# Four small changes of order in a two-layer trunk: x ahead of the first weights, a halving on ScalarE, copies ahead of low parts, mixing four places sooner

## The chip, the cores and the metric

The kernel runs on one core of one Trainium2 chip. The metric is the device time of one execution in microseconds (us), as the median of several runs. The profile is of one execution; its span is the time from the first to the last instruction that it shows. TensorE is PE (PEld its weight loads), VectorE DVE, ScalarE ACT, GpSimd POOL; SP issues nearly all DMAs.

## The reference

One sequence of 1024 tokens, width 1024, goes through two layers, all in fp32. Layer 0 mixes tokens with a gated MLP on one half of the width and a gated delta rule on the other; layer 1 with a differential attention. Both layers end with an MLP (width 4096, squared relu) and a gated embedding. What matters here is the start of layer 0 and the attention:

```python
hn = rms_norm(h, ln_mix_e[i])              # h = x
proj = hn @ w_in_e[i]                      # the first matmul
...
q = rms_norm(q.reshape(bsz, seq, C_HEADS, 2, C_HEAD_DIM), q_gain) * (C_HEAD_DIM ** -0.5)
k = rms_norm(k.reshape(bsz, seq, C_HEADS, 2, C_HEAD_DIM), k_gain)
slopes = alibi_slopes(C_HEADS)             # 2 ** -(1 .. 8) for the 8 heads
logits = jnp.einsum('bqhrd,bkhrd->bhrqk', q_blk, k) - slopes * dist
probs = softmax(where(dist >= 0, logits, -inf))
attn = probs[:, :, 0] - lam * probs[:, :, 1]
o = jnp.einsum('bhqk,bkhe->bqhe', attn, v)
h = h + rms_norm(o, sub_gain) * (1 - lam_init) @ w_out_o[i]
```

## The kernel before

Every fp32 operand of a large product is split into a rounded high part and the low rest, and a product is three matmuls (`mm3`: high by high, high by low, low by high). For a weight this is a DMA of a piece of 128 x 512 to `raw` (`Weight.load`, L103), a cast on ACT (L224) and a subtraction on DVE or POOL (L225). All instructions pass through a scheduler at build time, which orders each engine's instructions by the place at which the program emits them, by a model of when their operands are ready, and by what is marked as urgent; the order on each engine is then fixed. PE's matmuls all have line 78, its transposes line 81.

**Start.** `trunk` loads the first half of x (512 tokens) as two tiles of 128 x 2 x 1024, in four column pieces each (L2047, 256 KB a piece), and after each pair of pieces one of the four pieces of the first projection's weights (L2049, by L103). Below, these weight pieces are W0 to W3. `load_x` turns x by PE transposes into PSUM, eight times four of 128 x 128; ACT takes the scaled high part out of PSUM (L232), DVE the low part (L233), ACT also squares x for the norm (L849), and the turned x goes to memory by way of `xt` (L844, L845). Then come the second four weight pieces and all else that SP issues.

**Attention.** It works on 64 blocks, 8 heads by 8 blocks of 128 queries (block g is head g // 8, block b = g % 8 of it, with (b + 1) x 128 keys). One turn of the loop from L1212 on emits for block g the two logits (r = 0 and 1), the combination and the turning of block g - 1, the fetching of g - 2 and the values of g - 3.

- `logits`: two products into a PSUM bank (`qk`), one DVE instruction (L1065) that adds the table of distances `al` and keeps the row minimum `nm`, and an exponential on ACT (L1068). `al` is one SBUF tile of 128 x 1024; at the first block of each head it is multiplied by 0.5 in place (L1054), which gives the next head's slope.
- `begin` and `put_k`, `put_q`: a head's keys (queries) are turned by PE into one bank with the tag `tr`. ACT copies 64 partitions scaled (L1017; L1028 and L1029), then DVE writes the low part (L1018; L1030) from the same bank, for r = 0, and then the same for r = 1. ACT and DVE accesses of one PSUM bank are kept in the order in which the program emits them.
- Between these parts stand four calls of `pump` a turn. These are the numbered places: place i lies in block (i - 1) // 4. `pump` puts in a share of the projections for later heads as filler, by a table `MARKS` of (place, units done by then): 168 units are left when the loop starts, the last 16 are head 7's queries and keys. A unit is 12 matmuls of 256 columns; four units fill a bank with the tag `mm` (there are two), which is then evaluated by a square on ACT (L954), a sum and a root (L956 to L959) and two scalings on DVE (L963).
- From place 206 on (`TAIL`), `pump` also takes one step of `tails`: from 160 units on it turns the finished heads' outputs back (`put_halves`), and from 168 on it begins the output projection over heads 0 to 5 (`mix_part`, "mixing"): steps of six matmuls of 512 columns into an `mm` bank, whose weights are split by ACT and POOL and whose results are added to the residual on DVE (L1282). There are some 48 steps. What is left of them is emitted behind the loop, ahead of the rest of the output projection.

Of the kernel before, what the change touches and what calls it, by code (L numbers as in the profile page):

```python
# [13 lines left out]
AF = mybir.ActivationFunctionType  # L14
ALU = mybir.AluOpType
# [8 lines left out]
HT = 512  # L24
# [5 lines left out]
EARLY = 3000  # L30
LAG = 3
KA = (6, 5)
MARKS = ((64, 50), (192, 144), (212, 160), (227, 168))
TAIL = 205
LATE = {64: 5, 65: 2}
DIRECT = 61
# [5 lines left out]
def f32(ap):  # L42
    return ap.bitcast(F32)
# [73 lines left out]
class Trunk:  # L117
# [793 lines left out]
    def attention(self, w_qkv, w_out, gain_next, h_dram):  # L911

        nc = self.nc
        NB = NT
        hs, r = list(self.hs), list(self.r)
# [3 lines left out]
        al = self.slot("B", [P, S], F32, "al")  # L919
# [70 lines left out]
        half = (slice(0, 64), slice(64, P))  # L990
# [13 lines left out]
        def begin(hd):  # L1004

            qk = qks[hd]

            ks = self.slot(f"A{2 + hd % 2}", [P, 2, S], F32R, "ks")

            def put_k(hf):  # L1010
                pt = self.aux([P, HT], "tr", "tr")
                for t in range(4):
                    self.pe.transpose(pt[:, t * P : (t + 1) * P], qk[1][hf][:, t, :], self.ident)
                for r in range(2):
                    own, other = half[r], half[1 - r]
                    dst = ks[:, r, hf * HT : (hf + 1) * HT]
                    nc.scalar.activation(dst[own], pt[own], AF.Copy, scale=self.kg[own])  # L1017
                    nc.vector.scalar_tensor_tensor(dst[other], pt[own], self.kg[own], f32(dst[own]), ALU.mult, ALU.subtract)  # L1018

            def put_q(b2):  # L1020
                pt = self.aux([P, HT], "tr", "tr")
                for i in range(2):
                    self.pe.transpose(pt[:, i * P : (i + 1) * P], qk[0][b2 // 2][:, 2 * (b2 % 2) + i, :], self.ident)
                qh = self.slot(f"c{11 + b2 % 2}", [P, 2, 2 * P], F32R, "qh")
                ql = qlow[b2 % 2]
                for r in range(2):
                    own, other = half[r], half[1 - r]
                    nc.scalar.activation(qh[own, r], pt[own, 0 : 2 * P], AF.Copy, scale=self.qg[own])  # L1028
                    nc.scalar.activation(qh[other, r], pt[own, 0 : 2 * P], AF.Copy, scale=self.qg[own])  # L1029
                    nc.vector.scalar_tensor_tensor(ql[own, r], pt[own, 0 : 2 * P], self.qg[own], f32(qh[own, r]), ALU.mult, ALU.subtract)  # L1030
                return qh, ql

            put_k(0)
            heads[hd] = [ks, put_k, put_q, put_q(0)]

        class Block:
# [14 lines left out]
            def logits(me, r):  # L1051
                hd, b, n, nm, lg = me.hd, me.b, me.n, me.nm, me.lg[r]
                if b == 0 and r == 0:
                    nc.vector.tensor_scalar(al, al, 0.5, None, ALU.mult)  # L1054
                ks, _, _, (qh, ql) = heads[hd][:4]
                qs = slice((b % 2) * P, (b % 2 + 1) * P)
                nch = (n + HT - 1) // HT
                u0 = (NB - 1 - b) * P
                for c in range(nch):
                    k0, k1 = c * HT, min(n, (c + 1) * HT)  # L1060
                    ps = self.aux([P, HT], next(qk_tag), "qk")
                    self.pe.matmul(ps[:, : k1 - k0], lhsT=qh[:, r, qs], rhs=ks[:, r, k0:k1], start=True, stop=False)
                    self.pe.matmul(ps[:, : k1 - k0], lhsT=ql[:, r, qs], rhs=ks[:, r, k0:k1], start=False, stop=True)

                    nc.vector.tensor_tensor_reduce(  # L1065
                        out=lg[:, k0:k1], in0=ps[:, : k1 - k0], in1=al[:, u0 + k0 : u0 + k1], scale=-1.0,
                        scalar=3.0e38 if c == 0 else nm[:, r, 0:1], op0=ALU.add, op1=ALU.min, accum_out=nm[:, r, c : c + 1])
                nc.scalar.activation(lg[:, :n], lg[:, :n], AF.Exp, bias=nm[:, r, nch - 1 : nch], scale=-1.0, accum_out=me.sums[:, b, r : r + 1])  # L1068
# [107 lines left out]

        marks = [(0, 0), *MARKS]
        state = [0, 0]
# [852 lines left out]
def trunk(tc, x, p, ln_mix_e, w_in_e, gmlp_v_gain, gmlp_ws, gmlp_bs, gdn_conv, gdn_a_log, gdn_dt_bias, gdn_out_gain,  # L2031
          w_out_e, ln_mix_o, w_qkv_o, attn_q_gain, attn_k_gain, diff_lambda, attn_sub_gain, w_out_o, ln_mlp, w_mlp1,
          w_mlp2, ln_ple, w_ple_gate, w_ple_proj, masks, out):
    with ExitStack() as ctx:
        T = Trunk(tc, ctx)
        nc = tc.nc
# [4 lines left out]
        def rows(half):  # L2041
            tiles = [T.slot(("A1", "A2", "A4", "A5")[2 * half + u], [P, 2, D], F32, "x") for u in range(2)]
            n = 2 * D // HT if half == 0 else 2
            for c in range(n):
                cols = slice(c * D // n, (c + 1) * D // n)
                for u in range(2):
                    nc.sync.dma_start(tiles[u][:, :, cols], xs[half, u, :, :, cols])  # L2047
                if half == 0:
                    first.load()  # L2049
            return [tiles[t // 2][:, t % 2] for t in range(4)]  # L2050

# [7 lines left out]
        first = Weight(T, [(w_in_e[0][:, 1536:1792], 0)], KT, 256)  # L2059
        nc.scalar.dma_start(vr[0:8, 0:P], ln_mix_e[0].rearrange("(k p) -> k p", p=P))  # L2060
        x0 = rows(0)
        pt = T.aux_ps()
        T.pe.transpose(pt[:, 0:8], vr[0:8, 0:P], T.ident[0:8, 0:8])
# [9 lines left out]
        def rows_of_rest():  # L2073
            x1.extend(rows(1))
            vr = T.tmp()
            nc.vector.memset(vr[:, 0:P], 0.0)
            nc.sync.dma_start(vr[8:24, 0:P], ln_mlp.rearrange("l (k p) -> (l k) p", p=P))
            nc.sync.dma_start(vr[24:40, 0:P], ln_ple.rearrange("l (k p) -> (l k) p", p=P))
            nc.sync.dma_start(vr[40:48, 0:P], ln_mix_o[0].rearrange("(k p) -> k p", p=P))
            nc.sync.dma_start(vr[48:96, 0:P], gdn_conv[0].rearrange("t (m p) -> (t m) p", p=P))  # L2080
            nc.sync.dma_start(vr[96:100, 0:P], gmlp_bs[0])
            pt = T.aux_ps()
            T.pe.transpose(pt[:, 0:P], vr[:, 0:P], T.ident)
            nc.vector.tensor_copy(cols[:, 8:], pt[:, 8:P])
# [73 lines left out]
```

## Time and profile before

| | |
|---|---|
| timed runs, median (lowest to highest) | 2484.7 us (2482.77 to 2484.95) |
| the profiled execution | 2487.14 us |
| its span | 2485.4 us |
| DMA in it | 459.73 MB, mean 185 GB/s |
| the switch from head 6 to head 7 (`al` halved) | at 1627.9 us |
| mean granted clock of PE | 0.998 |

A row of a group gives line, engine, operation, output and input tiles, shapes and count, then busy time, mean ns of one, and idle time of the engine before them with what ended it. A row of the timeline gives start and length in us. In the chain each piece is what the next one waited for.

### The profile page before, as it was taken

What the parts mean: (1) busy time and instruction counts of PE and PEld (TensorE: products, weight loads), DVE (VectorE), ACT (ScalarE), POOL (GpSimd) and SP (SyncE); (2) the same over time, 40 slices, a digit from 0 to 9 for tenths busy, and PEclk for the clock granted to TensorE, in tenths of its full rate; (3) what the DMA queues carried; (4) which work ended last, traced back from release to release, by engine and by line L of the source; (5) the groups of instructions that cost most, each with busy time, mean ns of one, the idle gap of its engine ahead of it and who ended that gap; (6) DMA issues with size and microseconds to landing.
All of it is one profiled execution on the core that took longest, in us unless ns stands there. A gap on an engine that the chain in (4) does not pass through costs nothing.

```text
span 2485.4 us, 39881 instructions
## 1 busy us (share of the span) xinstructions
PE 2467.7 (99%) x13588; PEld 2106.4 (85%) x13588; DVE 1864.7 (75%) x3639; ACT 1291.2 (52%) x2591; POOL 324.0 (13%) x304
## 2 busy tenths in 40 slices
PE   9999999999999999999999999999999999999999
PEld 7998898888888887888899999988878888888887
DVE  7787877697667879566568888876886677787687
ACT  6553444464455435454366766664654555445553
POOL 0221331000000000000244443342000000000010
PEclk9999999999999999999999999999999999999999
DMA  8385645457556755553347776787465558657772
GB/s 246 114 255 118 172 150 178 140 175 245 161 178 238 256 184 191 187 173 115 119 97 171 163 173 153 192 215 245 155 218 192 180 185 288 215 182 218 231 245 86
DMA packets 539620, 459.73 MB, mean 185 GB/s; under 512 B 229524, under 2 KB 400920, under 8 KB 539416
## 3 DMA queue, kind: packets, MB, share of 16 engines
q1 hardware_dynamic: 513032, 451.93, 60.0%
q10 hardware_dynamic: 25360, 3.15, 0.8%
q0 software_dynamic: 1024, 2.10, 0.3%
q8 instruction: 107, 1.75, 0.3%
q14 instruction: 97, 0.79, 0.1%
HBM read 322.10 MB, written 134.96 MB: 184 GB/s over the span
## 4 chain that ended last, share of the span: by engine, by line
PE 93%; DVE 3%; DMA 2%; issue 1%; ACT 1%; SPq 0%; POOL 0%; DVEq 0%; ACTq 0%; POOLq 0%
PE mm L78 82%; PE po L78 3%; PE qk L78 3%; PE aux L78 2%; PE tr L81 1%; DMA raw<-in_w_mlp_dram 0%; DMA spill<-early 0%; PE pkq L78 0%; DVE raw L283 0%; PE pz L78 0%; PE py L78 0%; PE pks L78 0%; PE pgm L78 0%; PE pvn L78 0%; PE pab L81 0%
## 5 line engine op out<-in xcount | busy, mean ns | idle before, releaser
L224 ACT CAST w<-raw 128x512 fp32r<-128x512 f32 x598 | 365.0, 617 | 460.9 <-PE mm L78 387.0
L78 PE MATMUL mm<-g,w 128*128 128x512 f32 x2592 | 603.1, 394 | 1.0 <-DVE g L225 0.8
L78 PEld LDWEIGHTS mm<-g,w 128*128 128x128 f32 x2592 | 486.5, 188 | 115.2 <-DVE g L225 1.7
L78 PE MATMUL mm<-hi,w 128*128 128x512 f32 x1728 | 552.8, 397 | 0.0
L78 PE MATMUL mm<-w,hi 128*128 128x256 f32 (+2 forms) x2528 | 503.1, 294 | 1.4 <-ACT t L1585 1.0
L225 DVE TENSOR_TENSOR w<-raw,w 128x512 fp32r<-128x512 f32 (+1 forms) x510 | 346.6, 687 | 166.7 <-ACT w L224 156.4
L78 PEld LDWEIGHTS mm<-w,hi 128*128 128x128 f32 x2528 | 401.4, 188 | 16.5 <-ACT t L1585 1.2
L78 PEld LDWEIGHTS mm<-hi,w 128*128 128x128 f32 x1728 | 324.4, 188 | 73.6
L78 PE MATMUL mm<-w,lo 128*128 128x256 f32 (+2 forms) x1264 | 368.0, 292 | 0.0
L78 PE MATMUL mm<-lo,w 128*128 128x512 f32 x864 | 340.1, 394 | 0.0
L78 PE MATMUL mm<-t,w 128*128 128x512 f32 x1152 | 271.0, 394 | 0.4 <-ACT w L224 0.2
L78 PEld LDWEIGHTS mm<-t,w 128*128 128x128 f32 x1152 | 216.2, 188 | 51.9 <-DVE t L225 1.0
L78 PEld LDWEIGHTS mm<-w,lo 128*128 128x128 f32 x1264 | 237.8, 188 | 5.7
L78 PEld LDWEIGHTS mm<-lo,w 128*128 128x128 f32 x864 | 162.8, 188 | 36.6
L224 ACT CAST g<-graw 128x512 fp32r<-128x512 f32 x216 | 132.7, 617 | 43.2 <-DMA graw<-gd 16.4
L225 DVE TENSOR_TENSOR g<-graw,g 128x512 fp32r<-128x512 f32 x216 | 146.9, 684 | 9.9 <-DMA gd<-g 7.9
L1068 ACT ACTIVATE lg<-lg,nm 128x128 f32<-128x128 f32 (+7 forms) x128 | 99.2, 775 | 74.5 <-DVE nm L1065 73.5
L265 POOL TENSOR_TENSOR r<-ms,mhalf 128x4 f32<-128x4 f32 x12 | 12.5, 1043 | 943.1 <-DVE ms L263 916.5
L225 POOL TENSOR_TENSOR w<-raw,w 128x512 fp32r<-128x512 f32 (+1 forms) x88 | 116.0, 1336 | 138.2 <-ACT w L224 93.2
L349 ACT ACTIVATE g<-g 128x512 f32<-128x512 f32 x96 | 60.4, 632 | 110.8 <-DVE g L283 107.2
L1065 DVE CUSTOM_DVE_ANT_0 lg<-qk,al 128x512 f32<-128x512 f32 (+3 forms) x128 | 74.8, 587 | 27.6 <-PE qk L78 23.7
L78 PE MATMUL mm<-ohi,w 128*128 128x512 f32 x256 | 86.6, 401 | 0.0
(340 smaller groups left out, 3534.4 us busy)
## 6 DMA issues: line engine op xcount, KB each, us to landing
raw<-in_w_mlp_dram SPq DMA_DIRECT2D x352, 256.0 KB, 3.3
graw<-gd SPq DMA_DIRECT2D x224, 256.0 KB, 2.9
gd<-g SPq DMA_DIRECT2D x192, 256.0 KB, 3.2
raw<-in_w_ple_gate_dram SPq DMA_DIRECT2D x76, 256.0 KB, 3.5
acc<-h_dram SPq DMA_DIRECT2D x64, 256.0 KB, 4.3
keep<-in_w_mlp_dram SPq DMA_DIRECT2D x64, 256.0 KB, 4.3
raw<-in_w_in_e_dram SPq DMA_DIRECT2D x60, 256.0 KB, 3.7
h_dram<-acc SPq DMA_DIRECT2D x48, 256.0 KB, 2.8
```

What stands on the lines that cost most here:

```text
L78: self._next(self.engine.matmul(*a, **k))
L81: self._next(self.engine.transpose(*a, **k))
L224: self.nc.scalar.copy(hi, src)
L225: (lo_engine or self.nc.vector).tensor_tensor(lo, src, f32(hi), ALU.subtract)
L265: nc.gpsimd.tensor_tensor(r, ms, self.mhalf[:, 0:4], ALU.pow)
L349: nc.scalar.activation(g, src, AF.Relu)
L1065: nc.vector.tensor_tensor_reduce(out=lg[:, k0:k1], in0=ps[:, : k1 - k0], in1=al[:, u0 + k0 : u0 + k1], scale=-1.0, scalar=3.0e38 if c == 0 ...
L1068: nc.scalar.activation(lg[:, :n], lg[:, :n], AF.Exp, bias=nm[:, r, nch - 1 : nch], scale=-1.0, accum_out=me.sums[:, b, r : r + 1])
```

## The change

The first half of x is issued whole, and the four first weight pieces after it. The table of distances is halved by an ACT copy with scale 0.5 instead of a DVE multiplication. In `put_k` and `put_q` the copies of both r are emitted ahead of the low parts of both. The last entry of `MARKS` is (223, 168) instead of (227, 168), so the last eight units are done, and mixing begins, four places sooner.

```diff
-MARKS = ((64, 50), (192, 144), (212, 160), (227, 168))
+MARKS = ((64, 50), (192, 144), (212, 160), (223, 168))
...
                 for t in range(4):
                     self.pe.transpose(pt[:, t * P : (t + 1) * P], qk[1][hf][:, t, :], self.ident)
-                for r in range(2):
+                dsts = [ks[:, r, hf * HT : (hf + 1) * HT] for r in range(2)]
+                for own, dst in zip(half, dsts):
+                    nc.scalar.activation(dst[own], pt[own], AF.Copy, scale=self.kg[own])
+                for r, dst in enumerate(dsts):
                     own, other = half[r], half[1 - r]
-                    dst = ks[:, r, hf * HT : (hf + 1) * HT]
-                    nc.scalar.activation(dst[own], pt[own], AF.Copy, scale=self.kg[own])
                     nc.vector.scalar_tensor_tensor(dst[other], pt[own], self.kg[own], f32(dst[own]), ALU.mult, ALU.subtract)
...
                     nc.scalar.activation(qh[own, r], pt[own, 0 : 2 * P], AF.Copy, scale=self.qg[own])
                     nc.scalar.activation(qh[other, r], pt[own, 0 : 2 * P], AF.Copy, scale=self.qg[own])
+                for r, own in enumerate(half):
                     nc.vector.scalar_tensor_tensor(ql[own, r], pt[own, 0 : 2 * P], self.qg[own], f32(qh[own, r]), ALU.mult, ALU.subtract)
...
                 if b == 0 and r == 0:
-                    nc.vector.tensor_scalar(al, al, 0.5, None, ALU.mult)
+                    nc.scalar.activation(al, al, AF.Copy, scale=0.5)
...
                     nc.sync.dma_start(tiles[u][:, :, cols], xs[half, u, :, :, cols])
-                if half == 0:
+            if half == 0:
+                for _ in range(first.pieces):
                     first.load()
```

## The prediction, made before the result was known

> **What bounds the kernel now.** First the page's busy times, then the view of waits: what TensorE (PE) waited for, with us in total, times, longest.
>
> ```profile
> PE 2467.7 (99%) x13588; PEld 2106.4 (85%) x13588; DVE 1864.7 (75%) x3639; ACT 1291.2 (52%) x2591; POOL 324.0 (13%) x304
> ...
> PE aux L81 <- DMA x<-in_x_dram: 2.1, 1, 2.1
> PE tr L81 <- DVE ks L1018: 1.0, 1, 1.0
> PE qk L78 <- ACT qh L1029: 0.9, 1, 0.9
> PE po L78 <- DMA aT<-a_dram: 0.4, 1, 0.4
> PE tr L81 <- DMA ol<-o_dram: 0.3, 1, 0.3
> ```
>
> PE is busy in 2467.7 of 2485.4 us. No edit takes a matmul away, so an edit pays only where PE stands still or its clock is low. Of the 17.7 us of standing still, the places the diff can reach are these waits: the one for x at the start, and two in attention (1.0 and 0.9) that belong together. The table by stretches shows where:
>
> ```profile
> 1500.00:1600.00 100.00, 99.56 (x803) 97.28 (x802) 80.97 (x220) 67.02 (x173) 42.80 (x36) 1.00 0.72 169
> ...
> 1625.00:1630.00 5.00, 3.70 (x20) 2.56 (x18) 4.79 (x11) 3.22 (x9) 1.50 (x3) 1.00 0.83 252
> 1630.00:1635.00 5.00, 4.15 (x21) 4.05 (x22) 4.87 (x14) 3.46 (x12) 1.64 (x1) 0.66 0.89 140
> ```
>
> The columns are length, then busy time of PE, PEld, DVE, ACT and POOL, granted clock, DMA share, GB/s. PE loses 1.30 + 0.85 = 2.15 us in ten, while DVE is nearly full (4.79 and 4.87 of 5), and just behind it the clock is 0.66. This is the switch from head 6 to head 7, where the projections run out. The chain of waits there, and from the timeline the instructions that hold it (start, us, engine, line; in brackets the engine's idle time before it and what ended that):
>
> ```profile
> 1626.06 0.76 DVE ks L1018
> ...
> 1631.32 2.67 PE po L78 x12
> ...
> 1634.74 1.70 PE po L78 x14
> 1636.44 0.27 PE qk L78
> 1636.71 4.18 PE mm L78 x18
> ```
>
> ```profile
> 1619.72 0.28 PE L78 MATMUL mm<-w,lo 128*128 128x256 f32 x1
> ...
> 1623.48 0.68 ACT L1017 ACTIVATE ks<-tr,kg 64x512 fp32r<-64x512 f32 x1 [0.48 <-PE tr L81]
> ...
> 1626.84 0.68 ACT L1017 ACTIVATE ks<-tr,kg 64x512 fp32r<-64x512 f32 x1 [1.72 <-DVE ks L1018]
> ...
> 1628.11 0.58 ACT L954 ACTIVATE t<-mm 128x512 f32<-128x512 f32 x1
> ...
> 1634.80 0.38 DVE L963 TENSOR_TENSOR k<-mm,ssf 128x256 f32<-128x256 f32 x1
> ```
>
> Two things meet. The first copy of head 7's keys ends at 1624.16, but ScalarE's (ACT's) second copy from the same PSUM bank (L1017) waits 1.72 us for VectorE's (DVE's) low part of the first, which starts only at 1626.06. And the last product of head 7's projections ends near 1620.0, but its square (L954) stands behind that on ACT until 1628.11, and its scaling (L963) ends at 1635.18. Only then is its `mm` bank free for the mixing's second product, which starts at 1636.7. So PE has no filler from 1627 to 1636. The slow clock costs, over the twelve `po`, 2.67 - 12 x 1.70/14 = 1.2 us. **The hole is worth 2.15 + 1.2 = 3.4 us**, or 2.15 + 5 x 0.34 = 3.9 by the clock column; I use 3.4.
>
> **The change, part by part.**
>
> *x ahead of the weights.* SP's queue issues pieces of 256 KB: two of x, one of the weights, four times over. Six later x pieces now pass W0, and W0 takes the ninth place, W2's. Below: the timeline, the chain, W2 in the view by tile (ns, start, us to landing) and the clock in the table by stretches.
>
> ```profile
> 7.35 0.62 ACT L224 CAST w<-raw 128x512 fp32r<-128x512 f32 x1 [4.42 <-DMA raw<-in_w_in_e_dram]
> ...
> 8.09 1.38 PE L81 MATMUL aux<-ident,x 128*128 128x128 f32 x8 [2.06 <-DMA x<-in_x_dram]
> ...
> 9.22 0.95 PE L78 MATMUL mm<-hi,w 128*128 128x512 f32 x2
> ```
>
> ```profile
> 9.46 3.26 PE mm L78 x8
> 12.72 0.60 PE aux L81 x4
> 13.32 0.92 PE mm L78 x4
> 14.24 0.87 PE aux L81 x8
> 15.12 0.47 PE mm L78 x2
> 15.59 0.44 PE aux L81 x4
> 16.02 9.72 PE mm L78 x42
> ```
>
> ```profile
> L103 SPq DMA_DIRECT2D raw<-in_w_in_e_dram x1: 884/884/884, 5.2 to 5.2; - x1
> ...
> DMA to landing us min/median/max: 6.4/6.4/6.4
> ```
>
> ```profile
> 10.00:11.00 1.00, 1.00 (x4) 0.81 (x3) 0.72 (x3) 1.00 (x4) 0.00 (x0) 0.50 1.08 376
> ...
> 13.00:14.00 1.00, 1.00 (x7) 0.87 (x6) 1.00 (x3) 1.00 (x4) 0.00 (x0) 1.00 1.09 349
> ```
>
> W0 lands at 7.35 now. W2 is issued at 5.24 and lands 6.4 later, at 11.6; so will W0. With its cast (0.62) the first product starts near 12.3 instead of 9.22, 3.05 later. In return, the 16 transposes that now lie between products (0.60 + 0.87 + 0.44 = 1.9 us) are done before. Up to 16.02 PE does 15 products; then it runs on without a gap at 9.72/42 = 0.231 us each. All warm: 12.27 + 15 x 0.231 = 15.7, 0.3 early. Eight at the cold 3.26/8 = 0.41: 12.27 + 3.26 + 7 x 0.231 = 17.15, 1.1 late. All cold: 18.4, 2.4 late. Which it is depends on the clock, 0.50 at 10 to 11 and back by 13: the transposes from 9 to 12 should keep PE busy enough, so I take the middle of the first two, **+0.4** (-0.3 to +2.4). ACT may also put squares of x (L849) before W0's cast; the range has room for that. The next weights, the `xt` stores and x's second half keep their places on SP, so nothing else moves; from 16.02 on PE runs without a gap, so nothing gives a delay back.
>
> *Clock rule.* The row first: PE stood still 2.06 us before 8.09 and the clock read 0.50 at 10 to 11; 0.98 + 0.92 us near 1630 brought 0.66. The Trainium skill, "TensorE: Matmul & The Clock Gate", Part 1, wants about 3.4 us of idleness first. By it the products at the start would be warm (-0.3) and the hole would cost only its 2.15 us, 1.75 of which might go: about -2.1 altogether, inside the forecast's own range. The rows contradict it, so the sum keeps the clock terms.
>
> *The table halved on ACT.*
>
> ```profile
> L1054 DVE TENSOR_SCALAR al<-al x8: 675/682/695, 936.6 to 1627.9; 128x1024 f32<-128x1024 f32 x8
> ```
>
> ```profile
> L1068 ACT ACTIVATE lg<-lg,nm 128x1024 f32<-128x1024 f32 x16 | 18.4, 1150 | 11.0 <-DVE nm L1065 10.8
> ```
>
> ```profile
> 1307.85 1.15 ACT L1068 ACTIVATE lg<-lg,nm 128x1024 f32<-128x1024 f32 x1
> ...
> 1308.97 0.29 DVE L1065 CUSTOM_DVE_ANT_0 lg<-qk,al 128x128 f32<-128x128 f32 x1
> ...
> 1311.22 0.36 PE L78 MATMUL qk<-ks,qh 128*128 128x256 f32 x1
> ```
>
> Eight times DVE loses 0.68 us; ACT gains a 128x1024 pass, for which the 1.15 us exponential is the nearest row and an upper bound: 1.1. It is also a new crossing DVE to ACT to DVE. At the switch from head 0 to 1 (last rows) ACT starts the exponential at 1307.85; queued behind it, the halving would end near 1307.85 + 1.15 + 1.1 = 1310.1, and the new head's first row minimum (L1065) would start 1.1 us later than 1308.97. Behind it wait that product's PSUM bank and DVE. PE's next logits come at 1311.22, so 1.1 us of cover remain, made of projections. Nothing to 7 x 1.1 = 7.7 us; I take **0**, since PE is 99.56 of 100 busy around the last such switch but one. At head 7 it even takes 0.68 us off the full DVE.
>
> *Copies first, mixing sooner.* Keys: ACT, ACT, DVE, DVE instead of ACT, DVE, ACT, DVE from one bank; queries alike. No instruction is added; ACT's 1.72 us wait goes, and the square at 1628.11 can move up by about as much. The first low part now waits for both copies, one copy (0.68) more, which DVE's backlog hides: the second copy would end near 1624.9, before DVE gets there at 1626.06. The last eight units of filler are spread over 11 places instead of 15, and the mixing's first step comes at place 223 instead of 227, that is in block 55 instead of 56. With it the last projection's evaluation stands one block earlier on ACT and DVE, so the bank that opened at 1635.18 opens some microseconds sooner, and the 18 products of 1636.71 (4.18 us) can cover the hole. Mixing's loads and stores come four places sooner too, on DMA engines that are 0.83 to 0.89 busy there. What is late next is probably a wait of the size of the present `aT` one (0.4). So **-3.4 + 0.4 = -3.0** (-3.4 to 0). At the end the mixing has four steps less:
>
> ```profile
> 1701.43 1.04 PE L81 MATMUL tr<-ident,lg 128*128 128x128 f32 x8
> ...
> 1721.42 1.95 PE L78 MATMUL po<-aT,aT 128*128 128x128 f32 x16
> ```
>
> The last block is transposed at 1702.5 and used at 1721.4, so 19 us cover four steps of about 1.4 (six products of 0.231 each). Cost nothing.
>
> **Sum.** +0.4 + 0 - 3.0 = -2.6 us. The profiled execution took 2487.14 (span 2485.4 and 1.7 around it) and would take 2484.5. It lies 2.4 above the median of the timed runs, 2484.7; the same difference there gives **2482.1**.
>
> **Rivals.** *All of it closes.* The hole by the clock column (3.9), the two DMA waits at its sides (0.4 and 0.3), and a warm start (0.3): -4.9, **2479.8**; down to 2478 if the new order of issue also tightens other switches, up to 2481 if half of the small terms stay. For it: DVE, the full engine, is relieved in both ways at once. Against: PE is 99.56 of 100 busy ahead of the hole, so little is to be had outside it.
>
> *The halving becomes the wait* (slower). If ACT runs it behind the exponential and PE reaches a product that needs the held bank first, each of seven switches costs up to 1.1 us and the hole stays: 2484.7 + 0.4 + 7.7 = 2492.8; at five of seven, **2490.6**. It decides where the cover (at head 1, 1311.22 - 1310.1 = 1.1) falls to nothing. Against it: projections lie between at every switch but the last. The Trainium skill, "ScalarE: Activation LUTs", Rules for kernel authors, puts multiplications on VectorE, which is this rival's reason; its formula gives an estimate of 186 + 0.833 x 1024 = 1040 ns on ACT, and the trace agrees that DVE is faster (682).
>
> *It does not do what it says.* The bank still opens late because L954 stays behind other work on ACT, and the late W0 isn't made up: half of the hole stays, +2.4 - 1.5 = +0.9, **2485.6**.
>
> **Chances.** Forecast 0.45 (its own range 2480.5 to 2484), all closes 0.28, halving 0.16, nothing done 0.11. Some 0.2% of this kernel, 5 us, is what its measurement can tell from no change: below 2479.7, or above 2489.7. Faster: over half of the second case and a tail of the first, 0.21. Slower: most of the halving, a little of the last, 0.17. Same: 0.62. The range 2478.5 to 2489.7 leaves out about 0.06 below and 0.13 above.
>
> **What will show it.** Right: PE's waits for `ks` and `qh` near 1628 are gone and the clock stays at 1.00; the two L1017 copies of one call run back to back; L954 of the last projection comes within a few microseconds of its product; products at the start begin near 12.3 and are even with before at about 16. Wrong: ACT's casts of W0 behind squares of x, a clock of 0.50 beyond 13 us, L1065 waiting for ACT's halving with PE idle behind it, or a new wait of PE after 1640.

## The result: 13 us slower, and the profile after

| | before | after |
|---|---|---|
| median of 6 timed runs (lowest to highest), us | 2484.8 (2482.77 to 2485.13) | 2497.7 (2494.08 to 2500.18) |
| ratio, with its 95% interval | | 1.0054 [1.0041, 1.0067] |
| the profiled execution, its span | 2487.14, 2485.4 | 2496.59, 2494.9 |

The forecast was 2482.1; the time went the other way, to 15.6 us above it. PE's busy time, from the page of the changed kernel, is 2467.2, nearly that of before (2467.7). So the 9.5 us between the two profiled executions are PE standing still, now 27.7 of 2494.9 us instead of 17.7 of 2485.4.

```profile
PE 2467.2 (99%) x13588; PEld 2103.9 (84%) x13588; DVE 1865.9 (75%) x3631; ACT 1295.7 (52%) x2599; POOL 319.6 (13%) x304
```

The view of waits of the changed kernel says what PE waited for (us, times, longest):

```profile
PE po L78 <- DMA aT<-a_dram: 6.9, 7, 2.0
PE tr L81 <- DVE rs L1076: 3.1, 1, 3.1
...
PE mm L78 <- ACT w L224: 1.2, 2, 1.0
...
PE aux L81 <- DVE xt L844: 1.0, 1, 1.0
```

The waits for `ks` and `qh` are gone, as the change meant. In their place stand waits for `aT`, the turned tables that come back from memory (0.4 before), and one of 3.1 behind DVE. The transfers are not slower: the median from issue to landing of the 44 loads of `aT` of 256 KB is 3.3 us, 3.5 before. The table by stretches, before and then after, shows where:

```profile
1600.00:1650.00 50.00, 47.85 (x310) 43.29 (x309) 42.88 (x106) 34.00 (x84) 18.22 (x14) 0.97 0.84 206
...
1650.00:1710.00 60.00, 59.49 (x310) 49.10 (x309) 35.77 (x86) 30.86 (x70) 21.81 (x20) 1.00 0.80 233
```

```profile
1500.00:1600.00 100.00, 96.86 (x773) 93.92 (x773) 81.32 (x212) 68.60 (x174) 42.67 (x35) 1.00 0.68 157
1600.00:1650.00 50.00, 50.00 (x338) 45.74 (x337) 40.22 (x104) 31.80 (x77) 20.33 (x16) 1.00 0.83 220
1650.00:1710.00 60.00, 52.31 (x277) 42.87 (x275) 36.55 (x92) 31.01 (x73) 18.87 (x19) 1.00 0.80 228
```

The hole that the prediction priced is closed: no idle time from 1600 to 1650, clock 1.00. But 2.7 us more are lost before it (96.86 against 99.56), and 7.69 behind it instead of 0.51. At the hole itself everything the prediction asked for is there (timeline of the changed kernel):

```profile
1625.86 0.60 ACT L954 ACTIVATE t<-mm 128x512 f32<-128x512 f32 x1
...
1629.46 1.38 ACT L1016 ACTIVATE ks<-tr,kg 64x512 fp32r<-64x512 f32 x2 [1.99 <-PE tr L81]
```

The two copies of the keys run back to back (one row, x2), and the square L954 stands ahead of them, less than 2 us behind its last product.

**Stage lengths.** Single executions differ by 3 to 4 us in places that no edit touches, so the twenty profiled executions of this study are taken in groups. Three marks, which both kernels have: the first row of the tile `early` in layer 0, behind the start; the building of `al` (IOTA, L920), ahead of attention; the last addition to `acc` behind attention. From the view by tile, before and after:

```profile
L1723 ACT ACTIVATE early<-early,carved x64: 384/388/404, 115.9 to 143.8; 128x128 f32<-128x128 f32 x64
...
L920 POOL IOTA al<- x1: 988/988/988, 930.7 to 930.7; 128x1024 f32 x1
...
L283 DVE TENSOR_TENSOR acc<-acc,acc x24: 675/681/687, 500.3 to 1801.6; 128x512 f32<-128x512 f32 x24
```

```profile
L1725 ACT ACTIVATE early<-early,carved x64: 384/389/409, 117.9 to 145.0; 128x128 f32<-128x128 f32 x64
...
L920 POOL IOTA al<- x1: 988/988/988, 931.2 to 931.2; 128x1024 f32 x1
...
L283 DVE TENSOR_TENSOR acc<-acc,acc x24: 682/686/692, 499.7 to 1809.7; 128x512 f32<-128x512 f32 x24
```

| executions | mark | mean (lowest to highest), us |
|---|---|---|
| weights between the pieces of x as before, 12 | first `early` | 115.2 (113.5 to 116.4) |
| x whole on SP, all weights behind it, 4 | first `early` | 119.0 (117.9 to 119.8) |
| the same 12, and 4 | IOTA | 929.1 and 932.9 |
| queries in the order of before, 12, and q_own, 1 | IOTA to last `acc` | 870.0 (867.6 to 873.7) |
| queries changed, `MARKS` of before, 4 | IOTA to last `acc` | 874.2 (873.1 to 875.9) |
| queries changed and mixing sooner, 3 | IOTA to last `acc` | 878.9 (878.5 to 879.3) |

So, in the means, the start costs 3.8 us, which are still there at 930 us, and attention 8.9 us: 12.7 of the measured 12.9. The pair of executions shown above would not have told: it is 2.0 apart at the first `early` and only 0.5 at IOTA. The experiments say which edits these are.

### The profile page after: what moved, and what is told of

It reads as the page before. It is cut to its first block, busy times and chain, and to the rows that moved or that the text cites. A ratio compares the mean times of both kernels' runs of the same rounds, so it can differ in the third digit from the quotient of the medians.

```text
span 2494.9 us, 39854 instructions
## 1 busy us (share of the span) xinstructions
PE 2467.2 (99%) x13588; PEld 2103.9 (84%) x13588; DVE 1865.9 (75%) x3631; ACT 1295.7 (52%) x2599; POOL 319.6 (13%) x304
## 3 DMA queue, kind: packets, MB, share of 16 engines
q0 software_dynamic: 1024, 2.10, 0.4%
## 5 line engine op out<-in xcount | busy, mean ns | idle before, releaser
L1070 ACT ACTIVATE lg<-lg,nm 128x128 f32<-128x128 f32 (+7 forms) x128 | 99.2, 775 | 89.8 <-DVE nm L1067 89.0
```

## The experiments

Each time is the median of its runs (5 to 11), the ratio (with its 95% interval) is against the kernel before on the same chip, and a cost in us is worked out from the ratio unless the text says otherwise. Theory A: the halving is the wait. C: the order of the copies is. M: the place of mixing is. S: the start is.

### The four edits alone

**only_al**

```diff
-                    nc.vector.tensor_scalar(al, al, 0.5, None, ALU.mult)
+                    nc.scalar.activation(al, al, AF.Copy, scale=0.5)
```

> The kernel before, with the halving of the distances' table on ScalarE alone. Theory A (the halving is the wait: each head's first row minimum starts later, the blocks fall behind the filler, TensorE runs dry at the end): the heads' halvings drift later from head to head as in the changed kernel, by 5 us or more at head 7, and the time is 5 to 13 us above before. Theory C (the order of the copies does it): drift under 2 us, time within 2 us of before. Theory M (the mixing's place does it): as C here.

Measured 2487.4, 1.0011 [1.0003, 1.0020]: 2.7 us slower, less than A asks for and more than C does. The drift speaks against A: from IOTA to the last halving of `al` it is 697.9 us here and 697.2 before. Its attention (871.2 us by the stage marks) lies inside the spread of the first group, so no trace shows where the 2.7 us are.

**only_copies**: the diff of `put_k` and `put_q` as in the change (here the end of `put_q` only).

```diff
...
+                for r, own in enumerate(half):
                     nc.vector.scalar_tensor_tensor(ql[own, r], ...)
```

> The kernel before, with the copies of keys and queries ahead of the low parts alone. Theory C: the blocks drift behind the filler head by head, 5 us or more at head 7, and the time is 5 to 13 us above before. Theory A: drift under 2 us, the second key copy no longer waits for the low part, time 0 to 4 us below before. Theory M: as A here.

Measured 2490.3, 1.0021 [1.0012, 1.0030]: 5 us slower, as C puts it. Its sign is there too: from IOTA to the last halving it is 704.5 us, 7.3 more than before.

**only_marks**

```diff
-MARKS = ((64, 50), (192, 144), (212, 160), (227, 168))
+MARKS = ((64, 50), (192, 144), (212, 160), (223, 168))
```

> The kernel before, with mixing begun at place 223 instead of 227 alone. Theory M (fill used up four places too soon): TensorE stands still some 5 to 8 us between head 7's fourth block and the end, time 5 to 8 us above before, heads 1 to 6 at their old times. Theories A and C: the hole at the switch to head 7 closes, time 1 to 4 us below before.

Measured 2484.65, 1.0002 [0.9993, 1.0011]: nothing, which no theory had. The table by stretches says why there is no gain either:

```profile
1600.00:1650.00 50.00, 48.99 (x314) 43.80 (x313) 41.53 (x102) 32.10 (x81) 19.86 (x16) 1.00 0.87 216
1650.00:1710.00 60.00, 57.59 (x305) 47.67 (x304) 39.14 (x87) 31.42 (x71) 17.76 (x18) 1.00 0.82 244
```

Against before PE gains 1.14 us from 1600 to 1650 and loses 1.90 from 1650 to 1710. Even alone the entry moves idle time; it does not remove it.

**only_x**

```diff
-                if half == 0:
+            if half == 0:
+                for _ in range(first.pieces):
                     first.load()
```

> The kernel before, with x loaded whole ahead of the first weights alone. In every theory the first product starts near 13 us instead of 9.2, TensorE is about 2 us behind before at 100 us and level with it by 160 us, where other waits take up the delay; time within 1 us of before. If the start does cost: 2 us above before, and a trace that is 2 us behind all the way.

Measured 2489.36, 1.0020 [1.0012, 1.0029]: 5 us slower, where at most 2 were expected. The four effects add up to 13 us, the whole loss. That looked like an answer, and it was a coincidence, as the combinations below show.

### The start

In the changed kernel W0 is issued at 4.87 and lands 6.3 us later, at 11.2. First W0 in the view by tile, then the timeline of PE and that of ACT:

```profile
L103 SPq DMA_DIRECT2D raw<-in_w_in_e_dram x1: 469/469/469, 4.9 to 4.9; - x1
...
DMA to landing us min/median/max: 6.3/6.3/6.3
```

```profile
10.65 0.63 PE L81 MATMUL aux<-ident,x 128*128 128x128 f32 x4 [1.04 <-DVE xt L844]
11.46 0.66 PE L81 MATMUL aux<-ident,x 128*128 128x128 f32 x4 [0.18 <-ACT xt L844]
13.13 0.80 PE L78 MATMUL mm<-hi,w 128*128 128x512 f32 x1 [1.02 <-ACT w L224]
```

```profile
11.28 1.29 ACT L232 ACTIVATE hi<-aux,cols 128x512 fp32r<-128x512 f32 x2
12.44 0.65 ACT L224 CAST w<-raw 128x512 fp32r<-128x512 f32 x1
```

The turnings don't fill the time until W0 is there. They wait for PSUM banks, which ACT and DVE have not emptied yet (the wait for `xt`), and ACT, full since 6.07, gets to the cast 1.2 us after the landing. The first product starts at 13.13 instead of 9.22. The slow clock that follows here (the last section) is not needed for the loss: in only_x it read 1.00 in every us from 8 to 20, and its first `early` comes at 119.6. There PE stood still 0.70 us for W0's low part and, near 36, once more 1.71 for `xt`.

**x_two**: W0 behind two pairs of pieces of x, the others each a pair later.

```diff
-                if half == 0:
+                if half == 0 and c:
                     first.load()
+            if half == 0:
+                first.load()
```

> Before with the weights' first piece (W0) behind two pairs of pieces of x instead of one, so at the fifth place on SP's queue; in the changed kernel it is at the ninth. Theory S, its landing: W0 lands near 9 us instead of 7.3 (11.2 with x whole) and the loss is in proportion, 2 of the 5 us: 2486 to 2487. Theory S2, the urgent squares of x that ACT runs ahead of the cast: with two pairs landed ACT already has its squares in hand when W0 comes, so nearly the whole loss shows: 2488 to 2489. If the loss of x whole comes only from the cold clock behind the gap, there is no gap here and the time is that of before, 2484 to 2485.

Measured 2483.4, 1.0000 [0.9991, 1.0009]. Neither S (in proportion to the landing) nor S2 (the squares): the first product is 1.05 us later than before (9.22) and costs nothing, because the turnings ahead of it leave little gap (0.56 us). Its PE:

```profile
8.81 1.71 PE L81 MATMUL aux<-ident,x 128*128 128x128 f32 x8 [0.56 <-DMA x<-in_x_dram]
10.27 0.47 PE L78 MATMUL mm<-hi,w 128*128 128x512 f32 x1
```

**x_w0**: x whole on SP, W0 alone issued by ACT's queue (`load` takes the queue as an argument).

```diff
...
+            if half == 0:
+                for i in range(first.pieces):
+                    first.load(None if i else nc.scalar)
```

> Before with x whole ahead of the weights on SP as in the changed kernel, but the first weight piece alone issued by ACT's queue, so that it lands early. x whole alone cost 5 us; W0 behind two pairs cost nothing. Theory S3, the gap: with x whole PE runs out of turnings before W0's low and high parts are there (first product 13.05, a wait of 1.0 for the cast and 0.7 for the low part, and in one run the clock at 0.50 behind it); with W0 early PE has products to lay between the turnings and nothing is lost, 2483 to 2485. Rival S4, x whole itself: PSUM banks stay full because ACT's urgent squares and the copies to xt come with x, whenever W0 lands, and the rest of the weights are late anyway: 2487 to 2489.

Measured 2482.61, 0.9995 [0.9986, 1.0003]. With x whole and W0 early the loss is gone, so S3 holds and S4 falls: x ahead is harmless as long as W0 is early, and the late W0, with the gap that it brings, is the cost. W0 is even earlier than before (its cast starts at 5.82 instead of 7.35). PE lays products between the turnings again:

```profile
8.36 1.20 PE L78 MATMUL mm<-hi,w 128*128 128x512 f32 x2
9.36 1.05 PE L81 MATMUL aux<-ident,x 128*128 128x128 f32 x4
10.06 0.78 PE L78 MATMUL mm<-lo,w 128*128 128x512 f32 x1
```

### The halving

**al_split2**

```diff
-                    nc.vector.tensor_scalar(al, al, 0.5, None, ALU.mult)
+                    nc.vector.tensor_scalar(al[:, S - P :], al[:, S - P :], 0.5, None, ALU.mult)
+                    nc.scalar.activation(al[:, : S - P], al[:, : S - P], AF.Copy, scale=0.5)
```

> Before with the table halved in two parts: DVE halves the last 128 columns, which are all that the first block of a head reads, and ACT the other 896 at the same place. The halving whole on ACT cost 2.7 us. Theory A, the crossing (the first row minimum of a head waits for ACT): the wait is gone, 2483.5 to 2485. Rival, ACT's extra load of 8 x 1.0 us: it stays, 2486.5 to 2488.

Measured 2485.29, 1.0002 [0.9994, 1.0011]. The point is a little above what A puts here, but the interval overlaps that of only_al, so it is not settled that the crossing is the cost. Both traces, only_al first, have the same larger wait for `qh` at the last switch (2.5 and 2.2, 0.9 before), so that wait does not tell them apart:

```profile
PE qk L78 <- ACT qh L1029: 2.5, 1, 2.5
```

```profile
PE qk L78 <- ACT qh L1029: 2.2, 1, 2.2
```

### The copies

**only_keys**: `put_k` as changed, `put_q` as before.

```diff
+                dsts = [ks[:, r, hf * HT : (hf + 1) * HT] for r in range(2)]
+                for own, dst in zip(half, dsts):
                     nc.scalar.activation(dst[own], pt[own], AF.Copy, scale=self.kg[own])
...
```

> Before with the key half of the copies edit alone (put_k). The whole edit alone cost 5 to 6 us. Theory C1, the keys: both copies of 64 x 512 stand ahead of both low parts, so ACT's queue holds a second copy of 0.68 us where a row minimum's exponential could have run, and DVE gets its two low parts in one stretch of 1.5 us; at 15 calls this is the larger half: 2488 to 2489. Theory C2, the queries: keys cost nothing or gain the wait of 1.72 us at the last switch, 2483 to 2485, and the loss is found in the queries. Rival, any new fixed order: keys alone cost about half, 2487, without either place showing why.

Measured 2484.53, 1.0002 [0.9993, 1.0011]: nothing.

**only_queries**: `put_q` as changed, `put_k` as before.

```diff
+                for r, own in enumerate(half):
                     nc.vector.scalar_tensor_tensor(ql[own, r], ...)
```

> Before with the query half of the copies edit alone (put_q): four ACT copies in a row from one bank, then the two low parts. C2: 32 calls, and the first low part waits for two copies of 64 x 256 more than before, so the queries of the next two blocks are ready later: 2488 to 2490. C1: 2484 to 2486. Rival, any new order: about half, 2487.

Measured 2487.04, 1.0016 [1.0007, 1.0025]: 3.4 us by the medians, 4 by the ratio. So C2, the queries, although 2488 to 2490 was expected. There are 32 calls of `put_q`, and each now puts four copies of 0.47 us in a row ahead of the first low part. That any new order costs is ruled out: x_two, only_marks and only_keys move instructions too, at no cost.

**q_own**: own copies, both low parts, other copies.

```diff
+                for r, own in enumerate(half):
                     nc.scalar.activation(qh[own, r], ...)
+                for r, own in enumerate(half):
                     nc.vector.scalar_tensor_tensor(ql[own, r], ...)
+                for r in range(2):
+                    own, other = half[r], half[1 - r]
                     nc.scalar.activation(qh[other, r], ...)
```

> Before with put_q alone changed, in another order than in the changed kernel: ACT's two own copies (L1028, which the low parts need), then both low parts on DVE, then ACT's two other copies (L1029). The queries in the changed kernel's order alone cost 3.4 to 4 us. Theory C2a, the low parts stand behind four ACT copies of 0.47 us instead of two: here the first stands behind two as before, so nothing is lost, 2483 to 2485. Theory C2b, the two low parts of 0.49 us stand in one stretch on DVE, ahead of row minima and combinations: they still do, 2487 to 2488. A third outcome: the other copies now wait for DVE as the second r's copies did before, and a loss appears that neither names, above 2488.

Measured 2484.82, 1.0003 [0.9994, 1.0012]. For C2a, against C2b: on DVE the two low parts of a call run as one pair 29 times of 32 here, 32 times in only_queries and never in before, and the pair costs nothing here. The intervals of q_own and only_queries overlap a little, so this step is likely rather than certain. The rows say how four copies in a row can cost. ACT and DVE of the changed kernel behind the switch to head 6, where two exponentials (L1070) and a combination (L1076) are due:

```profile
1581.33 0.29 DVE L1067 CUSTOM_DVE_ANT_0 lg<-qk,al 128x128 f32<-128x128 f32 x1
...
1582.85 0.47 ACT L1029 ACTIVATE qh<-tr,qg 64x256 fp32r<-64x256 f32 x1 [1.99 <-PE qk L78]
1583.33 0.47 ACT L1030 ACTIVATE qh<-tr,qg 64x256 fp32r<-64x256 f32 x1
1583.81 0.51 ACT L1070 ACTIVATE lg<-lg,nm 128x256 f32<-128x256 f32 x1
...
1584.43 0.47 ACT L1029 ACTIVATE qh<-tr,qg 64x256 fp32r<-64x256 f32 x1
1584.92 0.40 ACT L1070 ACTIVATE lg<-lg,nm 128x128 f32<-128x128 f32 x1
...
1585.45 0.16 DVE L1076 RECIPROCAL rs<-sums 128x1 f32<-128x1 f32 x1 [3.83 <-ACT lg L1070]
```

Both row minima are done at 1581.6. But ACT stands 1.99 us at a copy of queries that must wait for a product of PE, the first exponential is queued behind two copies and the second behind a third, and DVE stands 3.83 us for the second exponential. The same place in q_own:

```profile
1575.40 0.94 ACT L1027 ACTIVATE qh<-tr,qg 64x256 fp32r<-64x256 f32 x2
...
1577.47 0.51 ACT L1070 ACTIVATE lg<-lg,nm 128x256 f32<-128x256 f32 x1 [1.12 <-DVE nm L1067]
...
1577.97 0.39 ACT L1070 ACTIVATE lg<-lg,nm 128x128 f32<-128x128 f32 x1
...
1578.59 0.16 DVE L1076 RECIPROCAL rs<-sums 128x1 f32<-128x1 f32 x1
1578.59 0.96 ACT L1032 ACTIVATE qh<-tr,qg 64x256 fp32r<-64x256 f32 x2
```

Here the exponentials stand ahead of the last two copies, and DVE doesn't wait. DVE's waits for an exponential ahead of a combination (1245 to 1680; us, times, longest), before and in the changed kernel:

```profile
DVE rs L1074 <- ACT lg L1068: 17.3, 25, 1.1
```

```profile
DVE rs L1076 <- ACT lg L1070: 21.4, 26, 3.8
```

A wait of this length is not in only_queries (18.5, 22, 2.0); with the keys changed as well it is there (only_copies 19.6, 20, 3.5). By the program's order a late combination is a late table, a late store and a late `aT`. No run isolates that chain, but PE's wait for `aT` (1220 to 1760) goes with it: 0.4 before, 1.5 in q_own, 2.2 in only_marks, 3.7 in only_queries, 6.9 in the changed kernel.

### In company

**no_marks**: the changed kernel with the old entry.

```diff
-MARKS = ((64, 50), (192, 144), (212, 160), (223, 168))
+MARKS = ((64, 50), (192, 144), (212, 160), (227, 168))
```

> The changed kernel with the old last entry of MARKS (227). Alone that entry changed nothing (2484.65 against 2484.3). If the effects only add up: 2497.5, as the changed kernel. Rival M, interplay: because the blocks lag here, filler that is used up four places sooner leaves PE waiting for aT between 1650 and 1700 (7.7 us); with the old entry half of that goes, 2493 to 2495.

Measured 2490.61, 1.0026 [1.0017, 1.0034], against 1.0054 of the changed kernel: the entry that costs nothing alone costs 7 us here, about twice what M expected. Its table by stretches:

```profile
1600.00:1650.00 50.00, 47.96 (x335) 44.21 (x334) 43.11 (x111) 34.05 (x84) 17.75 (x14) 1.00 0.83 219
1650.00:1710.00 60.00, 59.82 (x316) 49.69 (x315) 36.94 (x91) 31.22 (x74) 23.49 (x21) 1.00 0.84 241
```

From 1600 to 1710 PE works 107.78 us here, 102.31 in the changed kernel, 107.34 in before. Closing the hole of 2.04 opens one of 7.69: the filler that used to be there behind 1650 has been spent. Around 1690 of the changed kernel:

```profile
1690.32 1.04 ACT L1070 ACTIVATE lg<-lg,nm 128x896 f32<-128x896 f32 x1 [1.41 <-DVE nm L1067]
...
1692.71 0.69 DVE L1067 CUSTOM_DVE_ANT_0 lg<-qk,al 128x512 f32<-128x512 f32 x1 [2.48 <-DMA a_dram<-lg]
...
1693.60 0.63 PE L81 MATMUL tr<-ident,ol 128*128 128x128 f32 x4 [3.09 <-DVE rs L1076]
```

The next row minimum waits for the store of an earlier table, whose buffer it needs, and PE has nothing to lay beside that.

**copies_marks**

```diff
-MARKS = ((64, 50), (192, 144), (212, 160), (227, 168))
+MARKS = ((64, 50), (192, 144), (212, 160), (223, 168))
... (`put_k` as in the change)
+                for r, own in enumerate(half):
                     nc.vector.scalar_tensor_tensor(ql[own, r], ...)
```

> Before with the copies edit (keys and queries) and mixing four places sooner. Alone 2490.3 and 2484.65. If they only add up: 2490 to 2491. Theory M1, MARKS interacts with the lag that the copies bring: the 7 us that the entry costs in the changed kernel show here too, 2495 to 2498. If MARKS interacts with the halving instead: 2490.

Measured 2494.55, 1.0040 [1.0028, 1.0053], against 1.0021 of the copies alone: 9.8 us by the medians, with the same wait of 3.1 for DVE. M1, a little below its range: MARKS costs beside the copies. The two intervals still touch; the stage lengths (879.3 here, 875.9 in only_copies) and no_marks point the same way.

**al_marks**

```diff
+MARKS = ((64, 50), (192, 144), (212, 160), (223, 168))
...
+                    nc.scalar.activation(al, al, AF.Copy, scale=0.5)
```

> Before with the halving on ACT and mixing four places sooner. Alone 2487.4 and 2484.65. If they add up: 2487 to 2488. Theory M2, MARKS interacts with the lag that the halving brings (at the last switch above all): 2491 to 2495. M1: 2487 to 2488.

Measured 2485.03, 1.0003 [0.9994, 1.0013]. M2 falls, and so does the sum of single effects: the halving's 2.7 do not show either.

**al_copies**

```diff
... (`put_k` as in the change)
+                for r, own in enumerate(half):
                     nc.vector.scalar_tensor_tensor(ql[own, r], ...)
...
+                    nc.scalar.activation(al, al, AF.Copy, scale=0.5)
```

> Before with the halving on ACT and the copies edit. Alone 2487.4 and 2490.3, and the changed kernel without the MARKS entry, which has x whole as well, took 2490.6. If they add up: 2492.5 to 2493.5. If the two delays lie side by side (one wait hides the other): 2489 to 2491.

Measured 2488.98, 1.0017 [1.0008, 1.0027]; with the copies alone 1.0021. Beside the copies no cost of the halving shows.

**no_x**: the changed kernel with the weights between the pieces of x.

```diff
-            if half == 0:
-                for _ in range(first.pieces):
+                if half == 0:
                     first.load()
```

> The changed kernel with the weights between the pieces of x as before: the halving, the copies and MARKS. Theory S3 (a gap at the start whose delay nothing gives back): 5 us less than the changed kernel, 2492 to 2494. If the loss at the start and the losses in attention hide one another: 2495 to 2498.

Measured 2494.36, 1.0036 [1.0023, 1.0048]: x costs 3 us by the medians and 5 by the ratios beside the rest as well, though this interval and that of the changed kernel overlap.

**no_queries**: the changed kernel with `put_q` as before.

```diff
-                for r, own in enumerate(half):
                     nc.vector.scalar_tensor_tensor(ql[own, r], ...)
```

> The changed kernel with put_q as before (keys, halving, MARKS and x as changed). Theory C2a with M1: the queries' low parts behind four copies bring the lag, and MARKS costs only beside that lag; so both go and x's 3 to 5 us stay, with at most a part of the halving's 2.7: 2488 to 2491. If the keys or the halving are MARKS's partner as well: 2493 to 2496.

Measured 2486.03, 1.0009 [1.0000, 1.0018]. One line put back takes 11 us away, more than expected: the keys and the halving are not MARKS's partners. What is left is 2.2 us (0 to 4.5), less than the 3 to 5 that x cost alone, although its profiled execution has the late start (118.6 at the first `early`).

**mended**: all four edits in forms that cost nothing alone.

```diff
+MARKS = ((64, 50), (192, 144), (212, 160), (223, 168))
...
+                for own, dst in zip(half, dsts):
...
+                    nc.scalar.activation(al[:, : S - P], al[:, : S - P], AF.Copy, scale=0.5)
...
+                if half == 0 and c:
+                    first.load()
...
```

> All four edits in the form that cost nothing alone: W0 behind two pairs of x (the other weights after each further pair), the last 128 columns of the table halved on DVE and the other 896 on ACT, copies first for the keys only, and mixing four places sooner. If the effects add up and the three causes are right: 2483 to 2486, against 2497.5 of the changed kernel. If the loss came from moving instructions about at all: above 2488. If the hole at the last switch closes now that nothing delays the blocks: 2480 to 2482.

Measured 2484.18, 0.9998 [0.9989, 1.0007]: as the three causes have it. The gain that the closed hole was to bring does not come: PE works 106.73 us from 1600 to 1710, 107.34 before.

**w0_keys**: x_w0 and only_keys together.

```diff
...
+                for own, dst in zip(half, dsts):
...
+                    first.load(None if i else nc.scalar)
```

> Before with the two edits that looked best alone: x whole with W0 by ACT's queue (2482.61 against 2483.73) and copies first for the keys only (2484.53 against 2483.66). If the first is a gain: 2482 to 2483 where before takes 2484. If PE's idle time at the last switch, which neither removes, decides: 2484.

Measured 2482.14, 0.9995 [0.9986, 1.0004]. The lowest median of all, but its interval takes in no change: no version here is shown to beat the kernel before.

## Why the prediction was wrong, point by point

- **x ahead, +0.4 (to +2.4).** W0's landing was right (11.6 foretold, 11.2 measured). The step that failed is "the transposes from 9 to 12 should keep PE busy enough": they ran out and waited for PSUM banks, the cast came 1.2 late behind ACT's queue, and the clock was 0.50 from 14 to 16 in the changed kernel. The first product started at 13.13 instead of the 12.3 foretold. Measured 3.8 by the stage marks, 2 to 5 by the times. The list of wrong signs had the cold clock and the late cast, but the term's range ended at +2.4. "Nothing gives a delay back" was right in the means: they are 3.8 apart at 115 and at 930 us. That PE runs without a gap from 16 on held in the changed kernel, not in only_x.
- **The halving, 0.** Right for this kernel, where it meets the copies; alone it measured 2.7. The instruction's length was well bounded (1.1):

```profile
L1056 ACT ACTIVATE al<-al x8: 1042/1042/1059, 935.0 to 1637.7; 128x1024 f32<-128x1024 f32 x8
```

  By the Trainium skill, "ScalarE: Activation LUTs", What ACT_TABLE_LOAD costs, such an instruction takes 186 ns and 0.833 ns for each of 1024 elements, an estimate of 1040 ns; this row agrees. The rival that made the halving the wait had the right side, but less than half of the size (2490.6, at most 2492.8) and the wrong mechanism: the halving adds nothing to copies and MARKS (copies_marks 1.0040; no_x, which is these two with the halving, 1.0036).
- **Copies and MARKS, -3.0 (to 0).** This step failed, and by the most: attention measured +8.9. Its argument looked at one call of `put_k` at one switch, and dismissed the rest with "queries alike". But the queries have 32 calls, four copies each, and stand on ACT among the exponentials all through attention. "No instruction is added" was true and beside the point: what was added is a longer row on an engine that works in order, and who waits behind it was not asked. The range's upper end, 0, had no reason.
- **What is late next, 0.4.** The hole was closed as foretold, and the next wait was 7.69 us, not "a wait of the size of the present `aT` one". Filler was counted as if it were made by being moved; it was taken from behind 1650. Alone that costs PE 1.90 us there and gains it 1.14 ahead of it, which the times do not show (only_marks); beside late blocks it costs 7.
- **The tail, nothing.** Not tried by itself; from 1710 to 1760 PE is busy in 50.00 of 50 us before and after.

Still open: whether the halving's 2.7 us alone are the crossing, how the 4 us of the queries divide between exponentials behind the copies and low parts behind them, and how much of the start's loss is standing still and how much the slow clock.

## What to carry to other kernels

Before regrouping instructions so that one engine does several in a row, count the calls and list what stands behind the row on that engine: here two copies more in a row on ACT cost 4 us over 32 calls, though no instruction was added. Filler moved into one hole is missing in the next one, and whether that costs depends on the other edits: test in combinations, since four single effects that add up to the whole loss can do so by chance. A first weight may land later for free as long as PE has other work that does not wait for the same engines (here 1 us later cost nothing, 4 us later cost 3.8).

## What the runs showed of the hardware

After nearly the same gap ahead of the first product, the clock was 0.50 from 14 to 16 in the changed kernel and 1.00 in only_x (busy times of PE 1.17 and 1.25 in the two us from 10, 0.98 in both in the next two). First the changed kernel, then only_x:

```profile
12.00:14.00 2.00, 0.98 (x4) 0.78 (x3) 2.00 (x4) 2.00 (x5) 0.00 (x0) 0.76 1.10 360
14.00:16.00 2.00, 2.00 (x5) 1.23 (x5) 2.00 (x4) 2.00 (x6) 0.00 (x0) 0.50 1.13 351
```

```profile
12.00:14.00 2.00, 0.98 (x5) 0.67 (x4) 2.00 (x4) 2.00 (x5) 0.00 (x0) 1.00 1.09 365
14.00:16.00 2.00, 1.30 (x7) 0.89 (x6) 2.00 (x4) 2.00 (x6) 0.00 (x0) 1.00 1.13 354
```

The kernels with the weights between the pieces of x show the same. In their twelve profiled executions PE stands still 1.53 to 2.06 us before its turnings near 8; from 10 to 11 the clock then reads 0.50 in nine of them and 1.00 in three (2.06 us and 0.50 in before, 2.05 us and 1.00 in only_queries). So a gap of this size may or may not bring the slow clock, and a prediction has to leave room for both.
